# Hybrid attention and Fourier block on one core: form loads moved into the gate products, the modulation weight on GpSimd's queue, squares shared with VectorE, unread products in the start

## The chip, the core and the metric

The kernel runs on one core of one Trainium2 chip. Of its engines, TensorE (PE) multiplies matrices, VectorE (DVE) and ScalarE (ACT) work element by element, GpSimd (POOL) here does little besides issuing transfers, and SyncE (SP) only issues transfers. Each engine takes its instructions strictly in the order in which they stand, and semaphores hold an instruction back until its inputs are there. The metric is the time of one execution in microseconds. Before the change three runs took 1408.48, 1409.1 and 1411.9 us, a median of 1409.1 us.

## The reference

The reference is one layer over 512 latent tokens of width 2048, with 256 context tokens, in single precision:

```python
shift, scale, gate = jnp.split(silu_c @ w_ada[l] + b_ada[l], 3, axis=-1)
h = _modulate(_rmsnorm(xs, norm_g[l]), shift[:, None], scale[:, None])
...
p = h @ w_l
...
attn = _attention(q, jnp.concatenate([k, kc], axis=1), jnp.concatenate([v, vc], axis=1))
y = _merge(p[..., OFF_ZA:], attn, w_proj_a[l], w_proj_b[l], w_out[l])
new_xs = xs + gate[:, None] * y
...
return _rmsnorm(xs, final_g)
```

`_merge` holds the two sigmoid gates, each of width 2048, that multiply the projections of the attention branch and of the Fourier branch; the merged result goes through `w_o`.

## The kernel before

Every matrix product is made of three PE products (`mm3`, lines 219 to 223), because each operand is split into a high part, rounded by ACT (line 120, `whi` or `hh`), and the rest, subtracted by DVE (line 121, `wlo` or `hl`).

The order in which the instructions of an engine stand is not that of the text alone: the framework places the instructions of each engine when the program is built, by its own estimate of when inputs are there. A load that the text calls early can stand early or late in its queue, and a split can be placed ahead of another one. The places named below are those in the built programs.

The start (lines 336 to 465). SP loads x, transposed, in the pieces of `XCH`, then the modulation's weight `w_ss` (two pieces of 1 MB, `wada_load`, for each of 16 blocks `kb` of 128 channels, four buffers), and the first columns of `w_in` in small pieces (`w_start`). `squares` sums the squares of x: ACT squares two blocks, DVE adds them, PE sums over the channels with a matrix of ones (line 360). `rx` is the reciprocal root. `modulation(kb)` multiplies the conditioning vector with the weight on PE (`matvec`, line 387, two halves of 8 products), copies the sums out (`columns`, line 394), turns them with two transposes (line 397) and makes `shift` and `gain` of them (lines 399, 440, 441). `make_h` makes the block of h: `ht` on DVE (376), `hh` on ACT (377), `hl` on DVE (378). Then the products with `w_start` follow (`start_work`), 42 for each block.

The middle is the Fourier branch, the keys and values, and 48 steps of attention with other products between them (`fill`). During the attention `form_row` writes the forms to a scratch tensor in HBM, `f_d`: sums and differences of quarters of h, which the gate products need.

The gates (lines 988 to 1006). Each group of 512 gate columns is computed with seven products instead of eight of its quarters: `P1`, `Q5`, `P2`, `Q6`, `P7`, `Q3`, `Q4`, each of 4 weight pieces of 12 PE products. `P1` uses the weight in four buffers `R0` to `R3`, which SP loads; after its use further quarters are added onto `R` for the products `Q5`, `Q6` and `Q4`. For `Q5` SP loads the quarter into `wr` and DVE adds it (line 185); later ones are added by a transfer of GpSimd (line 194). `Q5` needs the form `Z5`, `Q6` `S2`, `P7` `S3` and `Q3` `S4`. The eight loads of the forms (four forms, two halves, 0.5 MB each, line 993) stand together on GpSimd's queue, ahead of the last `fill(64)`; each half is split between two pieces of the first group (`between`, line 59). The weights of `P2` in its second and third piece are split into `hh` and `hl` halves that the blocks of h no longer need.

The end (lines 1083 to 1206). The output product with `w_o` runs in the same seven products. `squares_of` collects the squares of the result in `ssq`, `rms` makes the reciprocal root of them, `scale_early` scales the first 256 tokens, and `last` does it for the last two blocks of 128 tokens. Line 1166 asks for the root function once, with no input that holds it back, so that its table is loaded at the start of the program.

Of the kernel before, what the change touches and what calls it, by code (L numbers as in the profile page):

```python
# [60 lines left out]
    f = {"P1": "Z5", "P2": "S2", "Q6": "S3", "P7": "S4"}.get(name)  # L61
    return [(f, pc - 1)] if f and g == 0 and pc in (1, 2) else []

XCH = [(0, 4), (4, 4), (8, 4), (12, 2), (14, 2)]


def start_pieces():
# [15 lines left out]
def block_kernel(ctx, tc, xT, ctxT, x, c_row, w_ss, w_gate, vecs, qkg, rope, dft_c, dft_s,  # L83
                 w_start, w_kv, w_m, w_g, w_pab, w_o, final_g, out):
    nc = tc.nc
# [23 lines left out]
    def uid(s):  # L109
        cnt[0] += 1  # L110
        return f"{s}{cnt[0]}"
# [218 lines left out]

    def wada_load(kb, h):
        w = pap.tile([P, 8, 256], F32, tag="wada", bufs=4, name=uid("wa"))
        nc.sync.dma_start(w, w_ss[kb, :, 8 * h : 8 * h + 8, :])
        return w

    for a, n in XCH:
# [14 lines left out]
    def squares(srcs, n, r, new, run=None):  # L351

        acc = bank2()
        for q in range(0, KK, 2):
            a, b = new(), new()
            for t, src in zip((a, b), srcs(q)):
                nc.scalar.activation(t, src, ACT.Square)
            nc.vector.tensor_tensor(a, a, b, op=ALU.add)
            if run is None:
                nc.tensor.matmul(acc[:, :n], ones, a, start=q == 0, stop=q == KK - 2)  # L360
            elif q == 0:
                nc.vector.tensor_copy(run, a)
            else:
                nc.vector.tensor_tensor(run, run, a, op=ALU.add)
        if run is not None:
            nc.tensor.matmul(acc[:, :n], ones, run, start=True, stop=True)
        nc.scalar.activation(r, acc[:, :n], ACT.Sqrt, bias=eps_t[:, 0:1], scale=1.0 / D)
        nc.vector.reciprocal(r, r)

    wada = {(0, 0): wada_load(0, 0), (0, 1): wada_load(0, 1)}  # L370
    while todo and len(ahead) < 3:
        start_load()

    def make_h(hi, lo, src, rr, kb, j, pool, n):
        tmp = pool.tile([P, n], F32, tag="htmp", bufs=2, name=uid("ht"))
# [12 lines left out]
                                 start=kk < 4, stop=kk >= KK - 4)  # L388
                kk += 1

    def columns(acc):

        o = pap.tile([P, 256], F32, tag="ada_o", bufs=2, name=uid("ado"))
        nc.vector.tensor_copy(o, acc[:, :256])
        sp = acc[:, 512:768]
        for i in range(2):
            nc.tensor.transpose(sp[:, P * i : P * i + P], o[:, P * i : P * i + P], ident)
        r = pap.tile([P, 2, 2], F32, tag="ada_r", bufs=2, name=uid("adr"))
        nc.vector.tensor_reduce(r, sp.rearrange("p (h g r) -> p h r g", h=2, g=4)[:, :, 0:2, :], axis=AX.X, op=ALU.add)
        return r  # L400

    def start_work():
        ends = {kb + nk for kb, nk in GROUPS}
# [31 lines left out]

    def modulation(kb):
        acc = bank2()
        matvec(acc, [wada.pop((kb, h), None) or wada_load(kb, h) for h in range(2)])
        sp = columns(acc)
        nc.vector.tensor_scalar(shift[:, kb, :], sp[:, 0, :], bada[:, kb : kb + 1], None, op0=ALU.add)  # L440
        nc.vector.tensor_scalar(gain[:, kb, :], sp[:, 1, :], bsc1[:, kb : kb + 1], ng[:, kb : kb + 1],
                                op0=ALU.add, op1=ALU.mult)

    rx = pap.tile([P, T], F32, name="rx")
    squares(lambda q: (xt[:, q, :], xt[:, q + 1, :]), T, rx, lambda: hm.tile([P, 2, T], F32, tag="h", name=uid("sq"))[:, 0, :])
    modulation(0)
# [522 lines left out]
    def slot(pool, shape, dt=F32):  # L969

        return pool.tile([P] + list(shape), dt, tag="h" if pool is hm else "f", bufs=KK, name=uid("s"))
# [17 lines left out]
    for i, f in enumerate(FORMS):  # L989
        forms[f] = [None] * 8  # L990
        for h in range(2):
            whole[f, h] = slot(fm, (4, 256)) if (i, h) < (3, 1) else new_ev().rearrange("p t (j c) -> p (t j) c", j=2)
            nc.gpsimd.dma_start(whole[f, h], f_d[i, :, 4 * h : 4 * h + 4, :])
    fill(64)
    pss.close()
    ps2 = ctx.enter_context(tc.tile_pool(name="ps2", bufs=1, space=PSUM, reuse_waits="tile"))
    for g in range(4):
        group = Group(g, forms, new_ev, gate_done, {"a": "x", "b": "y", "c": "x"})
        for name in ONE_GROUP:
            if (g, name) == (0, "Q5"):  # L1000
                hl_pools += range(MORE_HL)
            elif (g, name) == (3, "Q3"):
                raw_pools.pop()
            elif (g, name) == (3, "Q4"):
                hl_pools[:] = [p for p in hl_pools if not isinstance(p, int)]
            group.run(name)
# [74 lines left out]

    row = lambda l, j: l[j // 2][:, j % 2, None, :].broadcast_to([P, 2, 512])
    ssq = const.tile([P, 4, 5], F32, name="ssq")
    new_o = lambda: slot(fm, (2, 512))

    def squares_of(v, t, i):
# [76 lines left out]
        nc.vector.scalar_tensor_tensor(part(0), part(0), r, fgs[0][:, 0, :], op0=ALU.mult, op1=ALU.mult)  # L1163
        store(tok, 0)

    nc.scalar.activation(ssq[:, 0, 0:1], eps_t, ACT.Sqrt)
    nc.vector.memset(ssq, 0.0)

    jobs.insert(0, lambda: form("A22", 0))
    jobs += [lambda: load_rows(1), lambda: form("A12", 1), lambda: form("A22", 1)]  # L1170
# [21 lines left out]
    for name in ONE_GROUP:  # L1192
        if name == "Q5":
            jobs += [lambda: form("S2", 0), lambda: form("S2", 1)]
        elif name == "P2":
            jobs += [lambda: form("S3", 0), lambda: form("S3", 1)]
        elif name == "Q6":
            jobs += [lambda: form("S4", 0), lambda: form("S4", 1)]
        elif name == "Q3":
            prepare(last_group.X, 0, 1)  # L1200
        elif name == "Q4":
            prepare(last_group.Y, 1, 0)
        last_group.run(name)
# [84 lines left out]
```

## Time and profile before

| | |
|---|---|
| time of the runs, median (lowest to highest) | 1409.1 us (1408.48 to 1411.9) |
| the profiled execution's own time | 1406.39 us |
| its span | 1404.3 us |
| DVE busy | 896.2 us (64%) |
| ACT busy | 614.2 us (44%) |
| moved by DMA | 275.28 MB, a mean of 196 GB/s |
| PE in the chain that ended last | 89% of the span |

Times in the rows are microseconds from the start of the span. In the rows of the timeline stand the start, the time taken, the engine, the line of the kernel, the operation, what it writes and reads, how many instructions are put together, and in brackets how long the engine was idle before it and what ended that. In the windows stand the busy time of each engine (and its count of instructions), the granted clock of PE (1.00 is full speed), the busy share of the 16 DMA engines and what they moved. In the view of the waits stand the sum, the number and the longest one. PEld is the loading of a stationary operand on PE.

### The profile page before, as it was taken

The numbers are of one execution on the slowest core, as the hardware profiler recorded it, in microseconds if no ns is written. First come the engines' busy times: TensorE is split into PE (matmuls) and PEld (weight loads), VectorE is DVE, ScalarE is ACT, GpSimd is POOL, SyncE is SP. The second block draws the span as 40 slices with busy tenths as digits, with TensorE's granted clock in tenths as the row PEclk, the third lists the DMA queues.
The fourth block names the chain that finished last, engine by engine and source line by source line (L and its number), as shares of the span: only waits on it lengthen the run. The fifth ranks groups of instructions, "written<-read, shape, count | busy, mean of one in ns | idle before, by whom it ended". The sixth has DMA issues, their size and how long they took to land.

```text
span 1404.3 us, 17554 instructions
## 1 busy us (share of the span) xinstructions
PE 1358.6 (97%) x6842; PEld 1110.5 (79%) x6842; DVE 896.2 (64%) x1185; ACT 614.2 (44%) x837; POOL 91.6 (7%) x133
## 2 busy tenths in 40 slices
PE   6999999999999999999999699999999999999995
PEld 3667789888888888888887488888888888888874
DVE  4866596767866668666643767575866544437777
ACT  5322253534554444545553545453544333233544
POOL 0000000011100001000001000000010100000100
PEclk9999999999999999999999799999999999999998
DMA  9887553636543435434438898878898844244883
GB/s 367 323 322 269 189 168 121 183 120 184 165 143 99 134 113 155 130 99 127 136 119 324 252 258 232 262 226 240 284 265 304 326 151 137 87 135 152 181 230 127
DMA packets 73668, 275.28 MB, mean 196 GB/s; under 512 B 8433, under 2 KB 9073, under 8 KB 69105
## 3 DMA queue, kind: packets, MB, share of 16 engines
q1 hardware_dynamic: 56160, 212.54, 44.9%
q0 software_dynamic: 12240, 44.05, 13.1%
q10 hardware_dynamic: 5184, 17.57, 3.4%
q8 instruction: 53, 0.87, 0.3%
q14 instruction: 31, 0.25, 0.1%
HBM read 248.95 MB, written 25.17 MB: 195 GB/s over the span
## 4 chain that ended last, share of the span: by engine, by line
PE 89%; DMA 4%; DVE 3%; ACT 1%; issue 1%; SPq 0%; DVEq 0%; ACTq 0%
PE pb L221 12%; PE pb L222 12%; PE pb L223 12%; PE x L222 7%; PE x L223 7%; PE x L221 7%; PE y L223 6%; PE y L222 6%; PE y L221 6%; PE pd L221 3%; PE pd L223 3%; PE pd L222 3%; PE pd L916 2%; PE pd L387 2%; DMA wr<-in_w_g 2%
## 5 line engine op out<-in xcount | busy, mean ns | idle before, releaser
L121 DVE TENSOR_TENSOR wlo<-wr,whi 128x1024 fp32r<-128x1024 f32 x188 | 226.1, 1206 | 183.3 <-ACT whi L120 182.3
L120 ACT ACTIVATE whi<-wr 128x1024 fp32r<-128x1024 f32 x188 | 195.8, 1045 | 332.9 <-PE y L223 89.7
L221 PE MATMUL pb<-hh,whi 128*128 128x512 f32 x512 | 207.2, 407 | 2.3 <-ACT hh L377 2.3
L222 PE MATMUL pb<-hl,whi 128*128 128x512 f32 x512 | 201.8, 394 | 0.0
L223 PE MATMUL pb<-hh,wlo 128*128 128x512 f32 x512 | 201.4, 393 | 0.0
L222 PE MATMUL y<-wlo,s 128*128 128x512 f32 x348 | 135.9, 391 | 1.5 <-DVE wlo L121 1.5
L221 PE MATMUL y<-whi,s 128*128 128x512 f32 x348 | 135.9, 390 | 0.0
L223 PE MATMUL y<-whi,s 128*128 128x512 f32 x348 | 135.7, 390 | 0.0
L221 PEld LDWEIGHTS pb<-hh,whi 128*128 128x128 f32 x512 | 96.6, 189 | 23.2 <-ACT hh L377 3.4
L223 PEld LDWEIGHTS pb<-hh,wlo 128*128 128x128 f32 x512 | 96.4, 188 | 22.3 <-issue 1.7
L222 PEld LDWEIGHTS pb<-hl,whi 128*128 128x128 f32 x512 | 96.8, 189 | 18.0 <-issue 1.6
L222 PE MATMUL x<-wlo,s 128*128 128x512 f32 x248 | 96.9, 391 | 0.6 <-DVE wlo L121 0.6
L221 PE MATMUL x<-whi,s 128*128 128x512 f32 x248 | 97.1, 391 | 0.0
L223 PE MATMUL x<-whi,s 128*128 128x512 f32 x248 | 96.7, 390 | 0.0
L120 ACT ACTIVATE whi<-R 128x1024 fp32r<-128x1024 f32 x57 | 59.8, 1057 | 62.9 <-PE x L223 37.8
L121 DVE TENSOR_TENSOR wlo<-R,whi 128x1024 fp32r<-128x1024 f32 x57 | 69.2, 1221 | 25.8 <-ACT whi L120 25.8
L907 ACT ACTIVATE p<-pd,mx 128x768 f32<-128x768 f32 x48 | 43.1, 898 | 86.0 <-DVE mx L905 86.0
L222 PEld LDWEIGHTS y<-wlo,s 128*128 128x128 f32 x348 | 65.3, 188 | 16.4 <-DVE wlo L121 2.8
L221 PEld LDWEIGHTS y<-whi,s 128*128 128x128 f32 x348 | 65.3, 188 | 13.7
L223 PEld LDWEIGHTS y<-whi,s 128*128 128x128 f32 x348 | 65.3, 188 | 13.6
L121 DVE TENSOR_TENSOR ptl<-pd,pth 128x768 fp32r<-128x768 f32 x48 | 45.8, 954 | 30.1 <-ACT pth L120 30.1
L221 PE MATMUL pb<-whi,hh 128*128 128x512 f32 x144 | 57.1, 396 | 0.1
(278 smaller groups left out, 2687.1 us busy)
## 6 DMA issues: line engine op xcount, KB each, us to landing
wr<-in_w_g SPq DMA_DIRECT2D x80, 512.0 KB, 6.4
wa<-in_w_ss SPq DMA_DIRECT2D x32, 1024.0 KB, 7.8
wr<-in_w_m SPq DMA_DIRECT2D x44, 512.0 KB, 3.8
wr<-in_w_gate SPq DMA_DIRECT2D x32, 512.0 KB, 3.7
wr<-in_w_pab SPq DMA_DIRECT2D x32, 512.0 KB, 5.0
R<-in_w_g POOLq DMA_DIRECT2D x32, 512.0 KB, 9.2
wr<-in_w_o SPq DMA_DIRECT2D x32, 512.0 KB, 3.7
wr<-in_w_start SPq DMA_DIRECT2D x26, 512.0 KB, 6.6
```

Of the source, the lines that this page charges most:

```text
L120: nc.scalar.activation(hi, src, ACT.Copy)
L121: nc.vector.tensor_tensor(lo, src, hi.bitcast(F32), op=ALU.subtract)
L221: nc.tensor.matmul(o, ah, bh, start=start, stop=False, skip_group_check=cont)
L222: nc.tensor.matmul(o, ah, bl, start=False, stop=False, skip_group_check=cont)
L223: nc.tensor.matmul(o, al, bh, start=False, stop=stop, skip_group_check=cont)
L387: nc.tensor.matmul(acc[32 * j : 32 * j + 32, :256], c2[:, kk, :], w[:, k, :], start=kk < 4, stop=kk >= KK - 4)
L907: nc.scalar.activation(p, sc[:, :NKEY], ACT.Exp, bias=mx[:, 0:1], accum_out=mx[:, 1:2])
L916: nc.tensor.transpose(tp[:, k * P : (k + 1) * P], p[:, k * P : (k + 1) * P], ident)
```

## The change

1. x comes in six pieces instead of five, the first two of half the size.
2. The modulation's weight of blocks 2 to 15 is loaded on GpSimd's queue instead of SP's. The weight of block 1 is asked for beside that of block 0.
3. In the first stage three of the sixteen squares are made by DVE (a product with itself) instead of ACT. The sums leave PSUM through ACT instead of DVE (`columns`).
4. Eight PE products whose result nobody reads (`warm`) stand around the first modulation: three before its transposes, five after them.
5. The loads of `Z5` stay ahead of `fill(64)`; those of `S2`, `S3` and `S4` are asked for in the text at the start of `P1`, `Q5` and `P2`.
6. The table of the root function is asked for ahead of `Q3` of the output product, by an instruction that reads `ssq`; line 1166 goes, and `ssq` is cleared where it is allocated.

```diff
-XCH = [(0, 4), (4, 4), (8, 4), (12, 2), (14, 2)]
+XCH = [(0, 2), (2, 2), (4, 4), (8, 4), (12, 2), (14, 2)]
...
-        nc.sync.dma_start(w, w_ss[kb, :, 8 * h : 8 * h + 8, :])
+        (nc.gpsimd if kb > 1 else nc.sync).dma_start(w, w_ss[kb, :, 8 * h : 8 * h + 8, :])
...
-                nc.scalar.activation(t, src, ACT.Square)
+                if run is None and t is b and q in (4, 8, 10):
+                    nc.vector.tensor_tensor(t, src, src, op=ALU.mult)
+                else:
+                    nc.scalar.activation(t, src, ACT.Square)
...
-    wada = {(0, 0): wada_load(0, 0), (0, 1): wada_load(0, 1)}
+    wada = {(0, h): wada_load(0, h) for h in range(2)}
     while todo and len(ahead) < 3:
         start_load()
+    wada.update({(1, h): wada_load(1, h) for h in range(2)})
...
-        nc.vector.tensor_copy(o, acc[:, :256])
+        nc.scalar.copy(o, acc[:, :256])
         sp = acc[:, 512:768]
         for i in range(2):
             nc.tensor.transpose(sp[:, P * i : P * i + P], o[:, P * i : P * i + P], ident)
+        if kb == 0:
+            warm(5, o)
...
+    def warm(n, src):
+
+        for _ in range(n):
+            nc.tensor.matmul(wacc[:, :256], ones, src, start=True, stop=True)
...
-        matvec(acc, [wada.pop((kb, h), None) or wada_load(kb, h) for h in range(2)])
-        sp = columns(acc)
+        matvec(acc, pieces := [wada.pop((kb, h), None) or wada_load(kb, h) for h in range(2)])
+        if kb == 0:
+            warm(3, pieces[1][:, 7, :])
+        sp = columns(acc, kb)
...
+    wacc = bank()
...
-            whole[f, h] = slot(fm, (4, 256)) if (i, h) < (3, 1) else new_ev().rearrange("p t (j c) -> p (t j) c", j=2)
-            nc.gpsimd.dma_start(whole[f, h], f_d[i, :, 4 * h : 4 * h + 4, :])
+            if (i, h) < (3, 1):
+                whole[f, h] = slot(fm, (4, 256))
+
+    def load_form(i):
+        for h in range(2):
+            if (i, h) == (3, 1):
+                whole[FORMS[i], h] = new_ev().rearrange("p t (j c) -> p (t j) c", j=2)
+            nc.gpsimd.dma_start(whole[FORMS[i], h], f_d[i, :, 4 * h : 4 * h + 4, :])
+
+    load_form(0)
     fill(64)
...
         for name in ONE_GROUP:
+            if g == 0 and name in ("P1", "Q5", "P2"):
+                load_form(("P1", "Q5", "P2").index(name) + 1)
...
     ssq = const.tile([P, 4, 5], F32, name="ssq")
+    nc.vector.memset(ssq, 0.0)
...
-    nc.scalar.activation(ssq[:, 0, 0:1], eps_t, ACT.Sqrt)
-    nc.vector.memset(ssq, 0.0)
...
         elif name == "Q3":
+
+            nc.scalar.activation(mhalf[:, 8:9], ssq[:, 0, 2:3], ACT.Sqrt)
             prepare(last_group.X, 0, 1)
```

2 lines of the change are left out of this document (1 added, 1 removed).

## The prediction

> **What bounds the kernel now.** I read the page's head and its share of busy time first, then the list of waits of PE, then the windows, to see what each stage costs, and last the timeline of the three places where PE is not at full speed.
>
> ```profile
> span 1404.3 us, 17554 instructions
> PE 1358.6 (97%) x6842; PEld 1110.5 (79%) x6842; DVE 896.2 (64%) x1185; ACT 614.2 (44%) x837; POOL 91.6 (7%) x133
> ...
> PE x L221 <- ACT whi L120: 9.5, 2, 7.8
> ...
> PE x L222 <- DVE wlo L121: 7.4, 3, 6.0
> ```
>
> PE is busy for 1358.6 of 1404.3 us, so at most 45.7 us can be won without removing products or raising the clock. The waits (sum, number, longest) show that the two largest with a split at their end come to 16.9 us, and that single ones of 7.8 and 6.0 us make up most of it. The windows show where.
>
> ```profile
> 25.05:31.00 5.95, 5.95 (x26) 3.71 (x27) 1.87 (x4) 1.17 (x2) 0.00 (x0) 0.56 0.87 322
> ...
> 45.00:60.00 15.00, 14.91 (x98) 9.25 (x100) 13.17 (x25) 3.75 (x5) 0.00 (x0) 1.00 1.01 411
> ...
> 75.00:190.00 115.00, 115.00 (x737) 83.71 (x736) 70.34 (x121) 27.92 (x35) 0.00 (x0) 1.00 0.67 247
> ...
> 761.00:768.00 7.00, 5.67 (x26) 4.35 (x24) 1.82 (x2) 1.26 (x2) 0.00 (x0) 1.00 1.03 413
> 768.00:791.40 23.40, 8.46 (x23) 5.93 (x24) 19.19 (x19) 14.56 (x19) 0.90 (x1) 0.64 0.80 298
> ...
> 810.00:1000.00 190.00, 190.00 (x840) 157.30 (x839) 122.61 (x132) 92.73 (x113) 16.36 (x19) 1.00 0.87 248
> ```
>
> Columns are the stretch, its length, the busy time and count of PE, PEld, DVE, ACT and POOL, then the granted clock, the DMA share and GB/s. Between 75 and 190 us and between 810 and 1000 us PE is busy all the time at clock 1.00: nothing that only helps other engines there can shorten the kernel. Two stretches differ. From 25.05 to 31 us PE is busy but at a clock of 0.56. From 768 to 791.4 us it works 8.46 of 23.4 us, at 0.64, just after seven microseconds in which DMA was full (share 1.03). That second place is the start of the gates, and the largest thing to win. A PE product at full clock takes 190/840 = 0.226 us.
>
> **Forms and the first gate products (part 5).**
>
> ```profile
> 749.03 3.67 POOL L993 DMA_DIRECT2D s<-f_d  x7
> ...
> 761.07 0.39 PE L221 MATMUL x<-whi,hh 128*128 128x512 f32 x1
> ...
> 766.74 0.63 ACT L120 ACTIVATE hh<-wr 128x512 fp32r<-128x512 f32 x1 [5.77 <-DMA wr<-in_w_g]
> ...
> 770.45 1.15 ACT L120 ACTIVATE hh<-wr 128x512 fp32r<-128x512 f32 x2 [1.61 <-DMA wr<-in_w_g]
> ...
> 776.28 2.94 ACT L120 ACTIVATE s<-s 128x1024 fp32r<-128x1024 f32 x3
> 779.12 1.99 ACT L120 ACTIVATE whi<-R 128x1024 fp32r<-128x1024 f32 x2
> ...
> 784.60 1.23 DVE L185 TENSOR_TENSOR wr<-wr,wr 128x1024 f32<-128x1024 f32 x1 [1.82 <-DMA wr<-in_w_g]
> ...
> 785.74 1.22 DVE L121 TENSOR_TENSOR wlo<-R,whi 128x1024 fp32r<-128x1024 f32 x1
> ...
> 791.68 0.40 PE L221 MATMUL y<-whi,s 128*128 128x512 f32 x1
> ```
>
> P1 is 48 products, 48 × 0.226 = 10.9 us, and begins at 761.07. Q5's first product starts at 791.68, 30.6 us later, so 19.7 us are lost. The rows say how. ACT splits in order, and its split of R3 (`whi<-R`, 779.12) stands behind the splits of three halves of forms (`s<-s`, 776.28), which came late because seven form loads were issued together at 749.03. PE waited 7.8 us for that split. Then DVE's split of R3 (785.74) stood behind an addition of weights (784.60) that itself waited for a transfer, and PE waited 6.0 us more. Neither instruction ahead was needed for P1.
>
> The diff would spread the loads, but the built program does not: on GpSimd's queue seven of the eight form loads still stand together ahead of P1, and only the second half of `S4` moves, behind the four additions of line 194. So the burst of transfers stays; it even meets the stores of the forms' scratch a little sooner, and I charge 1 to 2 us of later landing for that. What does change is the order of the splits. On ACT, R3's `whi` now stands right behind the first of the `hh<-wr` splits and ahead of the other three and of `S2`. On DVE, R3's `wlo` stands ahead of the line 185 addition.
>
> ```profile
> L121 DVE TENSOR_TENSOR wlo<-wr,whi 128x1024 fp32r<-128x1024 f32 x188 | 226.1, 1206 | 183.3 <-ACT whi L120 182.3
> L120 ACT ACTIVATE whi<-wr 128x1024 fp32r<-128x1024 f32 x188 | 195.8, 1045 | 332.9 <-PE y L223 89.7
> ```
>
> A split costs 1.05 us on ACT and then 1.21 us on DVE. The replay: the first `hh<-wr` ended at 767.37 (766.74 + 0.63); with 1.2 us of delay 768.6. R3's `whi` ends at 769.6 and its `wlo` at 770.8. Line 221 needs the first, line 222 the second, so P1's last piece runs its second product at 770.8 and ends 11 products later, at 773.3, against 771.97 without a wait. Q5's first piece needs R0's new split, which on ACT stands behind the remaining three `hh<-wr` and the first half of `S2`. The last of these three ended at 771.6 before; 2 us later it is 773.6, then 2 × 1.05 us for `S2` and R0 gives 775.8, and DVE's 1.21 us gives 777.0. PE waits there about 3.4 us. Q5's third piece I let wait 0.8 us (its `whi` stands behind the second half of `S2`). Q5 then ends at 777.0 + 47 × 0.226 + 0.8 = 788.4. Before, it ended at about 791.68 + 10.9 = 802.6. That is 14.2 us.
>
> A wait of 3.4 us may bring the clock down. After a start with pauses the window from 25.05 shows 0.56 over 5.95 us, a loss of 0.44 × 5.95 = 2.6 us. I charge a dip as long as the wait that calls it, half of 3.4 us: 1.7 us; bounds 0 and 2.6. Remaining: 12.5 us. The bounds are 8 (the transfers come 4 us later still) and 19.7 (no wait left). The Trainium skill, "TensorE: Matmul & The Clock Gate", section "Part 1: The HAM clock gate (the "warmup" mystery)", says that activity is judged in free-running windows of about 3.4 us, an idle one bringing half rate and a busy one full rate. The trace agrees (0.56 and 0.64 stand behind its two idle places); by it alone the charge is either nothing or one window, an estimate of 1.7 us.
>
> The gain can only stay if later transfers keep up. From 810 to 1000 us the DMA share is 0.87 with PE never idle; 0.13 × 190 = 25 us of room, more than 12.5. So I expect no give-back.
>
> **The start (parts 1, 3, 4).**
>
> ```profile
> 6.22 2.19 ACT L357 ACTIVATE sq<-xt 128x512 f32<-128x512 f32 x4 [0.95 <-DMA xt<-in_xT]
> ...
> 8.15 9.63 PE L360 MATMUL pd<-sq,ones 128*128 128x512 f32 x16 [8.15 <-DVE sq L358]
> ...
> 17.82 0.69 ACT L367 ACTIVATE rx<-pd,eps_t 128x512 f32<-128x512 f32 x1 [2.38 <-PE pd L360]
> 18.53 3.35 DVE L368 RECIPROCAL rx<-rx 128x512 f32<-128x512 f32 x1 [2.38 <-ACT rx L367]
> ...
> 22.76 0.17 DVE L399 TENSOR_REDUCE adr<-pd 128x4 f32<-128x16 f32 x1 [0.59 <-PE pd L397]
> ...
> 23.43 0.75 DVE L376 SCALAR_TENSOR_TENSOR ht<-xt,gain,rx 128x512 f32<-128x512 f32 x1
> 24.10 1.22 DVE L121 TENSOR_TENSOR wlo<-wr,whi 128x1024 fp32r<-128x1024 f32 x1
> 24.28 0.72 ACT L377 ACTIVATE hh<-ht,shift 128x512 fp32r<-128x512 f32 x1 [2.49 <-DVE ht L376]
> 25.05 2.07 PE L221 MATMUL pb<-hh,whi 128*128 128x512 f32 x4 [2.33 <-ACT hh L377]
> 25.89 1.02 DVE L121 TENSOR_TENSOR wlo<-wr,whi 128x256 fp32r<-128x256 f32 x2
> ```
>
> A square costs 2.19/4 = 0.55 us on ACT and three leave it, 1.6 us; but the sums follow the arrival of x (the last ends at 17.78, ACT's root waits 2.38 us for it), and in the built order ACT loads the root's table within the squares instead of before them. So the root stays near 17.8 us, and the reciprocal still ends at 21.9. Behind it DVE has the chain sums, `gain`, `ht`. In the built order two splits that stood behind `ht` (24.10 and the pair at 25.89) now stand ahead of it: 1.22 + 1.02 = 2.24 us more, of which the time DVE idles there for PE's transposes takes back some; I put the first product at 26.4 instead of 25.05, a loss of 1.4.
>
> Against that stand three terms. In the wait PE does one half of block 1's `matvec`, whose weight now comes early: −1.07 (row below). The five unread products behind the transposes, which end at about 22.7 (the sum waits for them until 22.76), take 5 × 1.07/8 = 0.7 us or up to twice that at half clock and keep PE in use until about 23.8, so that of the 2.6 us of half clock some half goes: −1.2; by the skill's windows that would be none or one of them. And GpSimd's loads of block 2 share DMA with the rest of block 1 from about 18 us, which I charge with 0.4. Net 1.4 − 1.07 − 1.2 + 0.4 = −0.5; as the first product may come later still, I take −0.3. Bounds: all splits on the path and a colder clock, +3; no split on the path and all the clock, −1.07 − 2.6 + 1.4 = −2.3.
>
> **The modulation's weight on GpSimd's queue (part 2).**
>
> ```profile
> 42.76 1.07 PE L387 MATMUL pd<-wa,c 128*32 128x256 f32 x16
> ...
> 80.53 1.93 PE L387 MATMUL pd<-wa,c 128*32 128x256 f32 x32
> ...
> wa<-in_w_ss SPq DMA_DIRECT2D x32, 1024.0 KB, 7.8
> ...
> R<-in_w_g POOLq DMA_DIRECT2D x32, 512.0 KB, 9.2
> ```
>
> The two halves of a `matvec` (x16 each, two passes a product) cost 1.07 us when they stand apart, and 1.93 us together: 0.21 saved by each merge. In the built order there are 20 runs of them, not 25: 5 × 0.21 = 1.0 us. On GpSimd's queue nothing else of that time stands, so an issue that waits for a buffer holds up no one, and SP's loads of `w_start` no longer stand behind such an issue. PE has no wait to lose there. Moving the sums from DVE to ACT moves work to the engine that is busy 27.92 of 115 us in that stretch: nothing on the path. Bounds: −2 and the third rival.
>
> **The end (part 6).**
>
> ```profile
> 1386.83 1.28 ACT L1125 ACT_TABLE_LOAD   x1
> 1386.92 0.75 DVE L1152 TENSOR_TENSOR s<-y,s 128x256 f32<-128x256 f32 x2
> ...
> 1391.90 0.16 DVE L1124 TENSOR_REDUCE r<-ssq 128x1 f32<-128x5 f32 x1 [0.64 <-ACT s L1088]
> ```
>
> The table's 1.28 us leave the tail, but in the built order DVE's merge of `s` (1386.92), which ran beside that load, now stands behind the scaling of the first tokens that the load held up; the last square then ends near 1391.9 as now, and the reduction at 1391.90 moves by nothing. I take 0; bounds +0.3 and −1.28.
>
> **The sum.** −12.5 − 0.3 − 1.0 = −13.8. On the profiled execution's own 1406.39 us (span 1404.3 and 2.1 around it), which lies 2.7 below the median of the runs, that is 1392.6; on the median 1409.1 it is 1395.3 us.
>
> **The rivals.**
>
> First, part of the stall only moves. The line 185 addition (784.60) now stands ahead of the split of Q5's third piece. If its transfer lands as late as before, that split ends at 784.6 + 1.23 + 1.21 = 787.0 where PE wants it at 783.1: 3.9 us, and another dip of 1.7. Gain 13.8 − 5.6 = 8.2: 1401. For it: the burst of transfers is the same. Against it: their buffers come free sooner, as P1 ends sooner.
>
> Second, all that is lost goes: 19.7 us at the gates, 2.6 at the start, 1.0 of merges, 23.3 together: 1386. For it: no arithmetic forbids it. Against it: the burst is unchanged in the built order, and it alone lasts beyond P1's end.
>
> Third, slower than before: GpSimd's queue doesn't bring `w_ss` at the needed rate, and PE starves between 45 and 190 us. At 247 GB/s these 145 us want 35.8 MB. The gain is eaten once they take 13.8 us more, at 35.8/158.8 = 225 GB/s; at 215 GB/s they take 166.5, 21.5 more: 1395.3 + 21.5 = 1417. For it: transfers of half the size landed in 9.2 us from that queue against 7.8 from SP's. Against it: the window at 45 us moved 411 GB/s, and four buffers ask two blocks ahead. The Trainium skill, "DMA: Bandwidth & Descriptors", section "Queues, rings and completion order", says that each DMA engine takes turns between queues; by it SP's `w_start` gets half of what it had alone while both run, which speaks for this rival. No row of before has both queues loaded in that stretch.
>
> Fourth, the new order of splits isn't what decides: the transfers of R3 and of `wr` are, the 14 us stay, and the kernel does as before but for the merges and the start: 1408.
>
> **How the numbers follow.** The forecast has 0.60, the first rival 0.17, the second 0.07, the third 0.11, the fourth 0.05. Measurement tells 0.3% (4.2 us) from no change, so faster means below 1404.9. Forecast and the first two rivals lie there, 0.84, of which I move 0.01 to the others for spread; the fourth is the same, 0.05; the third slower, 0.11 and a mishap at the start beside it, 0.12 together. So 0.83, 0.05, 0.12. The range: the forecast's own is 1389 to 1400 by the bounds of the gates (8 to 19.7) and the start; it reaches up over the first rival to 1403.5 and leaves out the last two rivals and some of the second: 1388.5 to 1403.5.
>
> **What would show it.** Right: one wait of PE of 2 to 5 us at Q5's first piece instead of 7.8 and 6.0, Q5 ending 25 to 29 us after P1's start, against 41.5 before; `matvec` in 20 runs; first product of block 0 near 26.4; the reduction as far from the end as now. Wrong: PE waits for `wa` between 31 and 190 us (third rival); a wait of over 3 us on line 222 in Q5's third piece (first rival); R3's `whi` ending after 775 (fourth); form loads on GpSimd's queue held back in the run by something that the order doesn't show.

## The result, and the profile after

The changed kernel took a median of 1392.11 us in four runs (1391.06 to 1395.25), the kernel before beside it 1410.03 us (1408.48 to 1411.9). The ratio is 0.9876, with an interval of 0.9855 to 0.9897: 1.0 to 1.5% faster. The forecast was 1395.3 us in a range of 1388.5 to 1403.5. The profiled execution took 1392.62 us with a span of 1390.8, against 1404.3 before: 13.5 us less. By the medians the gain is more, 17.9 us where 13.8 was forecast, mostly because the profiled execution of the kernel before was 3.6 us faster than the median of its runs. The rows below account for the 13.5 us between the two profiles; a second profile of the changed kernel further down lies 17.6 us below the kernel before.

First the head of the page and the list of PE's waits of the changed kernel (sum, number, longest):

```profile
span 1390.8 us, 17626 instructions
PE 1358.8 (98%) x6858; PEld 1113.7 (80%) x6858; DVE 890.4 (64%) x1172; ACT 617.8 (44%) x849; POOL 106.6 (8%) x161
...
PE y L222 <- DVE wlo L121: 7.1, 5, 3.6
PE x L222 <- DVE wlo L121: 1.4, 2, 0.8
PE pb L221 <- ACT hh L381: 1.3, 1, 1.3
...
PE y L221 <- ACT whi L120: 0.6, 1, 0.6
```

PE is as long busy as before (1358.8 against 1358.6 us): the gain is idle time that went. The two waits of 7.8 and 6.0 us are gone. In their place stands one of 3.6 us on a `wlo`, for an accumulator `y`. The windows, with the columns as in the prediction:

```profile
25.00:31.00 6.00, 4.62 (x36) 2.53 (x29) 1.62 (x3) 2.68 (x5) 0.57 (x2) 1.00 1.02 419
...
768.00:791.40 23.40, 21.80 (x92) 17.16 (x93) 18.64 (x19) 16.39 (x18) 4.03 (x5) 1.00 1.05 329
791.40:810.00 18.60, 15.02 (x60) 11.95 (x59) 12.87 (x14) 9.27 (x11) 3.41 (x4) 0.91 0.84 231
```

The clock is 1.00 in the start, and PE works 21.80 instead of 8.46 us from 768 to 791.4 us. Part of the loss sits one window later now. The timeline there shows how:

```profile
758.15 0.39 PE L221 MATMUL x<-whi,hh 128*128 128x512 f32 x1
...
765.37 0.64 ACT L120 ACTIVATE hh<-wr 128x512 fp32r<-128x512 f32 x1 [2.46 <-DMA wr<-in_w_g]
765.91 1.04 ACT L120 ACTIVATE whi<-R 128x1024 fp32r<-128x1024 f32 x1
...
766.99 1.23 DVE L121 TENSOR_TENSOR wlo<-R,whi 128x1024 fp32r<-128x1024 f32 x1 [0.55 <-ACT whi L120]
...
772.86 0.50 PE L222 MATMUL y<-wlo,s 128*128 128x512 f32 x1 [0.76 <-DVE wlo L121]
...
785.25 1.06 ACT L120 ACTIVATE whi<-R 128x1024 fp32r<-128x1024 f32 x1
...
796.44 1.23 DVE L185 TENSOR_TENSOR wr<-wr,wr 128x1024 f32<-128x1024 f32 x1 [8.77 <-DMA wr<-in_w_g]
797.59 2.35 DVE L121 TENSOR_TENSOR wlo<-R,whi 128x1024 fp32r<-128x1024 f32 x2
...
798.86 0.50 PE L222 MATMUL y<-wlo,s 128*128 128x512 f32 x1 [3.58 <-DVE wlo L121]
...
811.26 0.39 PE L221 MATMUL x<-whi,s 128*128 128x512 f32 x1
```

R3's `whi` (765.91) stands right behind the first `hh<-wr`, and its `wlo` follows at 766.99, so P1 loses 1 us. Q5's first piece (second product at 772.86) loses 1.7 us, in waits of 0.55 and 0.76 us and the product between them. But Q6's first piece waits 3.58 us: its `whi` was ready at 786.3, and its `wlo` (797.59) stood on DVE behind an addition of two weights of P7 (796.44) that waited 8.77 us for a transfer. That is the mechanism which the prediction gave to its first rival, two of the seven products later than placed there (Q6 instead of Q5). Behind the wait PE's clock fell (0.91 in the window from 791.4): some nine products started 0.43 us apart instead of 0.23, which costs another 1.7 us.

A measure for the whole place: from P1's first product to P7's first stand 192 products, 192 × 0.227 = 43.6 us. Before they took 63.3 us (761.07 to 824.33), after 53.1 (758.15 to 811.26). The loss fell from 19.7 to 9.5 us. Of the 9.5, Q6's first piece has 5.5 (the wait and the clock), Q5's 1.8, P1's last piece 1.3; small delays make up the rest. The row of before:

```profile
824.33 0.39 PE L221 MATMUL x<-whi,s 128*128 128x512 f32 x1
```

The 13.5 us, in order of time: P1 begins 2.9 us sooner (761.07 to 758.15); 10.2 us at the gates; 1.2 us lost in the output product's P7, where PE's wait on line 222 grew; 1.7 us won behind the last product. For the last two the rows, first of the kernel before, then of the changed one:

```profile
1361.18 0.50 PE L222 MATMUL y<-wlo,s 128*128 128x512 f32 x1 [0.66 <-DVE wlo L121]
...
1389.37 9.83 SPq L1130 DMA_DIRECT2D out_y<-s  x14
...
1390.87 0.39 PE L223 MATMUL y<-whi,s 128*128 128x512 f32 x1
```

```profile
1347.02 1.23 DVE L185 TENSOR_TENSOR wr<-wr,wr 128x1024 f32<-128x1024 f32 x1 [6.36 <-DMA wr<-in_w_o]
1348.16 1.22 DVE L121 TENSOR_TENSOR wlo<-wr,whi 128x1024 fp32r<-128x1024 f32 x1
...
1349.43 0.50 PE L222 MATMUL y<-wlo,s 128*128 128x512 f32 x1 [1.88 <-DVE wlo L121]
...
1375.99 10.70 SPq L1155 DMA_DIRECT2D out_y<-s  x14
...
1379.08 0.39 PE L223 MATMUL y<-whi,s 128*128 128x512 f32 x1
...
1379.84 0.16 DVE L1149 TENSOR_REDUCE r<-ssq 128x1 f32<-128x5 f32 x1 [0.64 <-ACT s L1113]
```

The last product starts 13.4 us before the end in the kernel before and 11.7 in the changed one. The stores of the result begin 3.1 us ahead of it, against 1.5. At 1347 us the same pattern stands again: an addition that waits for a transfer, ahead of a split that PE wants.

### The profile page after: what moved, and what is told of

The parts are those of the page before. It is cut to its first block, busy times and chain, and to the rows that moved or that the text cites. A ratio compares the mean times of both kernels' runs of the same rounds, so it can differ in the third digit from the quotient of the medians.

```text
span 1390.8 us, 17626 instructions
## 1 busy us (share of the span) xinstructions
PE 1358.8 (98%) x6858; PEld 1113.7 (80%) x6858; DVE 890.4 (64%) x1172; ACT 617.8 (44%) x849; POOL 106.6 (8%) x161
## 4 chain that ended last, share of the span: by engine, by line
PE 89%; DMA 5%; DVE 4%; ACT 1%; issue 1%; DVEq 0%; SPq 0%; ACTq 0%
PE pb L221 12%; PE pb L222 12%; PE pb L223 12%; PE x L222 7%; PE x L223 7%; PE x L221 6%; PE y L222 6%; PE y L223 6%; PE y L221 6%; PE pd L221 3%; PE pd L223 3%; PE pd L222 3%; PE pd L930 2%; PE pd L391 2%; DMA wr<-in_w_g 2%; DVE wlo L121 1%
## 5 line engine op out<-in xcount | busy, mean ns | idle before, releaser
L222 PE MATMUL pb<-hl,whi 128*128 128x512 f32 x512 | 200.7, 392 | 0.1
## 6 DMA issues: line engine op xcount, KB each, us to landing
R<-in_w_g POOLq DMA_DIRECT2D x32, 512.0 KB, 10.1
```

The source lines that it names most:

```text
L222: nc.tensor.matmul(o, ah, bl, start=False, stop=False, skip_group_check=cont)
```

## The experiments

All were run beside the kernel before, whose median there was 1406.8 to 1407.7 us; so ratios to it are compared, also where two variants ran on different chips. Part 1, x in six pieces, was not tried alone. "Loss" is the time from the last product ahead of P1 to P7's first product less 0.227 us for each, taken from the trace (19.7 before, 9.5 in the changed kernel's first profile).

| kernel | us | ratio | interval | loss at the gates |
|---|---|---|---|---|
| changed kernel, again | 1388.74 | 0.9875 | 0.9860 to 0.9889 | 7.8 |
| before, with part 5 alone | 1394.03 | 0.9909 | 0.9892 to 0.9926 | 7.4 |
| part 5 undone | 1399.85 | 0.9941 | 0.9926 to 0.9957 | 17.4 |
| S3, S4 on SP's queue | 1389.36 | 0.9873 | 0.9853 to 0.9892 | 6.5 |
| part 6 undone | 1390.71 | 0.9880 | 0.9864 to 0.9897 | 7.9 |
| modulation's weight on SP | 1391.16 | 0.9887 | 0.9873 to 0.9902 | 7.3 |
| no unread products | 1391.57 | 0.9890 | 0.9874 to 0.9907 | 9.6 |
| nor their bank | 1391.71 | 0.9890 | 0.9875 to 0.9905 | 9.6 |
| part 3 undone | 1391.11 | 0.9885 | 0.9869 to 0.9902 | 7.6 |
| Q6's split ahead | 1386.94 | 0.9859 | 0.9844 to 0.9873 | 5.1 |
| three edits | 1384.83 | 0.9842 | 0.9828 to 0.9857 | 5.0 |
| the same, no unread products | 1388.72 | 0.9873 | 0.9858 to 0.9887 | 8.1 |

**The changed kernel again**

> The changed kernel itself, to stand beside the other three on the same chip: 0.987 to 0.989 of the kernel before. The loss around the first gate products (9.6 us in its first profile) and its places may differ from one execution to the next, as transfers land a microsecond sooner or later.

The ratio is the same, 0.9875. The loss was 7.8 us instead of 9.5: the wait at Q6 was 1.1 us instead of 3.6 there. So a difference of 2 us in this loss between two profiles says nothing by itself. The first product came at 25.6 us instead of 26.74, and the 588th, which is used below as a mark of the start, at 197.5 instead of 197.4.

**Part 5 alone, and all but part 5**

```diff
 kernel before:
+    load_form(0)
     fill(64)
...
+            if g == 0 and name in ("P1", "Q5", "P2"):
+                load_form(("P1", "Q5", "P2").index(name) + 1)
```

> The kernel before with part 5 alone (form loads asked for at P1, Q5 and P2). In its built program the splits around P1 stand in the same order as in the changed kernel: whi of R3 ahead of three of the four hh<-wr and of S2, wlo of R3 ahead of the line 185 addition of two wr. Theory A, that this order is the gain at the gates: 9 to 11 us faster than before, 1399 to 1401 us, PE's two waits of 7.8 and 6.0 us gone and one of 3 to 4 us at Q6's first piece (line 222), as in the changed kernel (19.7 us lost around the first products there, 9.6 after). Rival B, that part of the gain comes from the start or the queue of the modulation's weight (another phase of the clock, stores that leave sooner): less than 7 us faster, and a wait of more than 2 us still at R3.

The gain was 0.9%, 12.7 us by the medians (1406.76 to 1394.03), more than the 9 to 11 expected and close to the 12.5 that the prediction had summed for this part. The loss at the gates fell from 19.7 to 7.4 us, with the start and the queues of the kernel before, so rival B falls. Its waits:

```profile
PE y L222 <- DVE wlo L121: 3.2, 4, 1.4
...
PE x L221 <- ACT whi L120: 2.3, 1, 2.3
PE x L222 <- DVE wlo L121: 1.1, 2, 0.6
```

The reverse, in the changed kernel:

```diff
-    load_form(0)
+    for i in range(4):
+        load_form(i)
     fill(64)
...
-            if g == 0 and name in ("P1", "Q5", "P2"):
-                load_form(("P1", "Q5", "P2").index(name) + 1)
```

> The changed kernel with part 5 undone: all eight form loads ahead of the last fill(64), as before. In its built program whi of R3 stands again behind the four hh<-wr and the splits of S2 and S3. Theory A: 9 to 11 us slower than the changed kernel, 1401 to 1403 us, with PE waits of 6 to 8 us on whi<-R and 5 to 7 us on wlo<-R. Rival B: 1392 to 1397 us.

The size is theory A's: 17.4 us of loss at the gates against 7.8, and 0.0066 in the ratio, 9.3 us. The place is not what was expected, so this run doesn't confirm the mechanism. No split of R3 was waited for by 6 to 8 us; P1's very first product waited instead. Timeline of this run:

```profile
761.77 0.63 ACT L120 ACTIVATE hh<-wr 128x512 fp32r<-128x512 f32 x1 [6.05 <-DMA wr<-in_w_g]
...
765.39 1.99 ACT L120 ACTIVATE s<-s 128x1024 fp32r<-128x1024 f32 x2
...
767.28 1.54 ACT L864 COPY ev<-pb 128x512 f32<-128x512 f32 x3
...
768.87 0.79 PE L221 MATMUL x<-whi,hh 128*128 128x512 f32 x1 [12.89 <-ACT ev L864]
```

P1's accumulator waits for the copies of line 864 out of PSUM, which stand on ACT behind the `hh<-wr` that wait for a transfer and behind two splits of forms (`s<-s`). In the kernel before they stood there too, and no one waited. What differs is that the bank for the unread products (`wacc`) is taken ahead of all others. The likely account is that this moves the accumulators that are allocated later, and P1's now takes over a bank that those copies empty; the trace shows the copy that PE waits for and not the bank. (A run below takes the bank out of a variant that waits like this.) If so, part 4 put a wait into the program that only the new order of part 5 keeps short.

**The burst of transfers**

```diff
-            nc.gpsimd.dma_start(whole[FORMS[i], h], ...)
+            (nc.sync if i > 1 else nc.gpsimd).dma_start(whole[FORMS[i], h], ...)
```

> The changed kernel with the loads of S3 and S4 on SP's queue. ACT and DVE keep the order of the changed kernel, but three of these loads now stand behind P2's and P7's first weights and land later, so the burst of seven loads at 746 us is cut to four. Theory A, that the order of the splits sets the time: within 1.5 us of the changed kernel (1391 to 1394), and the wait at Q6's first piece stays, or grows because weights of P7 stand behind the forms. Rival C, that the burst itself still costs: R3 and the wr pieces land 3 us or more sooner, the waits of 0.6 to 0.8 us at R3 and at Q5's first piece go, 1387 to 1390 us.

0.9873 against 0.9875: theory A by the ratio. (1389.36 us would lie in rival C's range, but the changed kernel itself took 1388.74 when it was run again.) PE, ACT and DVE have exactly the order of the changed kernel. The loads of `S3` and the first half of `S4` were issued 11 to 15 us later, and the later pieces of weight landed sooner for it, the sixth at 769.2 instead of 773.3 us in the changed kernel run again. But the piece that ACT waits for first, the third, landed at 764.0 instead of 764.4. The wait at Q6 was 2.2 us, between the 1.1 and 3.6 of the changed kernel's two profiles. So the transfers did move as rival C says, the early ones least, and brought no time that can be measured. The order of the splits was the same in both, and so was the time.

**The table of the root (part 6)**

```diff
-            nc.scalar.activation(mhalf[:, 8:9], ssq[:, 0, 2:3], ACT.Sqrt)
...
+    nc.scalar.activation(ssq[:, 0, 0:1], eps_t, ACT.Sqrt)
+    nc.vector.memset(ssq, 0.0)
```

> The changed kernel with part 6 undone: the root's table is asked for at the start, and loaded anew in the end when the first root is wanted. By my forecast the chain up to the last sum of squares sets the end: same within 0.3 us. What the trace of the changed kernel shows instead: the first of the sixteen stores of the result starts 3.1 us ahead of the last product there and 1.5 us before, so the stores have drained when the last of them is issued: then 1.2 to 2 us slower with the part undone, 1393 to 1394 us, and the last store lands 5.8 us after the last scaling began instead of 4.3.

The ratios (0.9880 and 0.9875) don't differ beyond their intervals, though the median is 2.0 us higher (1390.71 against 1388.74). The traces show a smaller effect than expected: the last product starts 12.4 us before the end with the part undone, and 11.8 in both profiles of the changed kernel; 0.6 us. The last store lands 11.4 us after that product started against 10.8, which is these 0.6 us; in the eleven profiles with part 6 it lands after 10.5 to 10.9. The stores begin 1.5 us ahead of the last product, as in the kernel before:

```profile
1375.23 10.05 SPq L1154 DMA_DIRECT2D out_y<-s  x14
```

The 13.4 us of the kernel before, and of part 5 alone, are another 1.0 us longer. There the last store lands 11.7 us after the last product started, and the span goes on for 1.7 us behind that landing, against 1.0 with part 6 undone and in the changed kernel. So 0.27 us of it is the landing, and 0.76 lies behind all work. The 0.76 aren't part 6's: the run with the modulation's weight on SP, which has part 6, shows them too (1.7). In these three profiles one packet of the instruction queue arrives just before the end, and it doesn't in the changed kernel's two. The Trainium skill, "ScalarE: Activation LUTs", section "What ACT_TABLE_LOAD costs", gives 1.28 us for the load and 1.38 more for a drain. The trace has the 1.28 us, but no run here shows the drain, and the end came only 0.6 us sooner.

**The queue of the modulation's weight (part 2)**

```diff
-        (nc.gpsimd if kb > 1 else nc.sync).dma_start(w, w_ss[...])
+        nc.sync.dma_start(w, w_ss[...])
```

> The changed kernel with the modulation's weight of blocks 2 to 15 on SP's queue again (the weight of block 1 still asked for early). In the built program the matvec products stand in 23 runs, against 20 in the changed kernel and 25 before. Theory A, that GpSimd's queue brings only the merges (0.2 to 0.3 us each) and nothing waits for it: 0.5 to 1.0 us slower than the changed kernel. Rival D, that the queue itself is worth more since loads of w_start no longer stand behind weight loads that wait for buffers: 2 us or more slower, with PE waits in the first 75 us. Rival E, my third one in a small form, that two queues take bandwidth from each other: same or faster.

The ratio rose by 0.0012, within the intervals; by the medians the run is 2.4 us slower, which alone would fit rival D. The trace says that the start doesn't differ: of PE's products on lines 221 to 223 the 588th, by which all 16 blocks of `matvec` are done, started at 197.5 us in both, though one had 20 runs of `matvec` and the other 23. PE waits there for no weight, and once 0.5 us for a copy at 53 us. So neither the queue nor the merges are worth anything in the start that shows, and rival D falls with its place, the first 75 us; the 2.4 us are not explained. The Trainium skill, "DMA: Bandwidth & Descriptors", section "Queues, rings and completion order", has each DMA engine take turns between its queues; no run here shows a price of such turns in the start. The same product started at 200.7 us in the kernel before.

**The unread products (part 4)**

```diff
-        if kb == 0:
-            warm(3, pieces[1][:, 7, :])
...
-        if kb == 0:
-            warm(5, o)
```

> The changed kernel without the eight unread products. In its built program DVE makes ht of the first block right after gain, and the three wlo splits stand behind it, as before. Theory A, that the unread products pay by the clock: the granted clock falls to 0.5 to 0.7 somewhere between 22 and 31 us, the first product with w_start comes 1 to 2 us sooner (25 to 25.7 instead of 26.7), and the sum is 0 to 1.5 us slower than the changed kernel. Rival F, that they cost more than they pay, as they push ht behind the splits: the clock stays at 1.00 without them since block 1's weight is there early and keeps PE in use, and the kernel is 1 to 2 us faster.

The first product comes sooner and the clock dips, as theory A had it:

```profile
24.40 2.07 PE L221 MATMUL pb<-hh,whi 128*128 128x512 f32 x4 [3.40 <-ACT hh L381]
...
25.00:31.00 6.00, 6.00 (x34) 4.19 (x33) 1.26 (x3) 2.49 (x5) 0.53 (x1) 0.81 1.01 416
```

Both cancel: the 588th product starts at 197.3 us, against 197.5 with them. Yet the kernel is 2.8 us slower by the medians (1391.57 against 1388.74; the intervals overlap). Part of the loss lies 560 us later: P1's first product waits for the copy of line 864, and in all 1.8 us more are lost at the gates. Another 2.3 us of this profile lie in the output product's P7, whose wait is 3.1 us here and 1.1 in the changed kernel run again.

```profile
759.82 0.50 PE L221 MATMUL x<-whi,hh 128*128 128x512 f32 x1 [3.05 <-ACT ev L864]
```

So the next run took the bank away too.

```diff
-    wacc = bank()
```

> The changed kernel without the eight unread products and without the PSUM bank that is taken for them ahead of all others. Without the products alone the start was as fast by the 588th product (197.3 us against 197.5) and the kernel 2.8 us slower; there P1's first product waited 3.0 us for the last copy of line 864, whose bank its accumulator takes over. With the bank gone too, P1's accumulator lies in banks that transposes used, as in the kernel before. Theory H, that the slower time was the bank and not the clock: the wait at P1's start goes, and the time is that of the changed kernel within 1 us or better, 0.9865 to 0.988 of the kernel before. Rival A, that the unread products pay by the clock: 0.9885 to 0.99, as without the products alone.

The wait at P1's start went, as theory H says, which shows that the bank made it, but the time did not come back: 0.9890 again, and a loss of 9.6 us, now with 2.9 us at Q6's first piece and 1.4 at Q5's. The 588th product stood at 197.7 us. The pair below repeats it: 8.1 us are lost at the gates without unread products and 5.0 with them. In the three variants without them the loss is 8.1 to 9.6 us, in the eight profiles with them and part 5 it lies between 5.0 and 9.5; the kernel before with part 5 alone, which never had them, lost 7.4. Theory H isn't borne out as an account of the time; the intervals of 0.9890 and 0.9875 overlap, and those of the pair below don't. That the products pay by the clock of the start isn't shown either, since the start is as fast without them. Nor is a fall of the clock at the gates bound to their absence: five of the eight profiles with them have one, of 0.86 to 0.93 in the window from 768 or the one from 791.4 us. By what way they change the gates stays open.

**Q6's split ahead of the addition**

```diff
+            if e.key[:2] == ("P7", 0) and e.key[2] > 1:
+                nc.vector.scalar_tensor_tensor(src, src, zero, r, op0=ALU.add, op1=ALU.add)
...
+        if e.key == ("Q6", 0, 1):
+            nc.vector.tensor_scalar(zero, lo[:, 0:1].bitcast(F32), 0.0, None, op0=ALU.mult)
```

> The changed kernel in which the additions of two weights for the third and fourth piece of P7 (line 185) also add a zero that DVE makes of Q6's second split, so that DVE cannot take them ahead of Q6's first two splits; the result is the same. Theory A, that Q6's first piece waits only because DVE's split of R0 stands behind an addition that waits for a transfer: the wait of 3.6 us on line 222 there goes, and the clock's dip behind it: 3 to 5 us faster than the changed kernel. Rival G, that the transfers bound this stretch (DMA share 1.05 from 768 to 791 us), so that the stall only moves on to the first products of P7: within 1.5 us of the changed kernel.

Q6's `wlo` now come at 786.24, the addition at 797.28, and PE has no wait at Q6's first piece:

```profile
786.24 2.35 DVE L121 TENSOR_TENSOR wlo<-R,whi 128x1024 fp32r<-128x1024 f32 x2
...
793.53 0.39 PE L227 MATMUL y<-whi,s 128*128 128x512 f32 x1
793.75 0.39 PE L228 MATMUL y<-wlo,s 128*128 128x512 f32 x1
...
797.28 1.28 DVE L187 SCALAR_TENSOR_TENSOR wr<-wr,zero,wr 128x1024 f32<-128x1024 f32 x1
```

The loss is 5.1 us, 2.7 less than the changed kernel's on the same chip, and the time 1.8 us less (1386.94 against 1388.74; its slowest run is faster than the other's fastest). The mechanism is shown: with the order turned round the wait is gone. The expected 3 to 5 us were too many, because that wait was 1.1 us in that chip's trace and not 3.6. The rest of the 2.7 us is not the edit's: behind Q5's first piece the changed kernel's profile has some nine products at half rate, and this one has none. And 2.7 us went lost again in the output product's P7, where PE's wait was 2.6 us instead of 1.1 and the clock fell behind it.

**Three edits together**

```diff
-    wacc = bank()
     squares(...)
+    wacc = bank()
...
+            if e.key[:2] == ("P7", 0) and e.key[2] > 1 or e.key == ("P7", 4, 3):
+        if e.key in (("Q6", 0, 1), ("P7", 4, 2)):
```

> The changed kernel with three edits: the bank of the unread products is taken behind the first stage's sums, so that P1's accumulator lies as before; the zero of Q6's second split in the additions for P7's last two pieces of the first gate group; and the same for the addition for P7's last piece of the output product, behind which DVE's split of the third piece stood (PE wait of 1.9 us at 1349 us). Theory A: no wait at Q6's first piece nor in the output product's P7, 3 to 5 us faster than the changed kernel, 0.984 to 0.986 of the kernel before. Rival G, that transfers bound both places: 0.987 or more.

> As a_best, without the unread products and their bank. Theory H: like a_best within 1 us, as the products pay nothing by themselves. Rival A: 2 us or more slower than a_best.

0.9842 is the fastest, 22.9 us below the kernel before; it and the changed kernel run again, on another chip, are 3.9 us apart (0.9842 and 0.9875). What each of the three edits brings here was not tried, but for Q6's above. The largest wait at the gates and behind is 0.8 us:

```profile
PE y L228 <- DVE wlo L121: 2.9, 5, 0.8
PE x L228 <- DVE wlo L121: 1.5, 2, 0.8
```

Without the unread products it is 3.9 us slower, and the slowest of four runs with them is faster than the fastest without. The windows from 768 to 791.4 us, with and without them, show where the clock dips, and the rows show Q5's first product:

```profile
768.00:791.40 23.40, 21.81 (x94) 17.15 (x93) 20.10 (x21) 15.67 (x17) 5.73 (x7) 1.00 1.05 324
...
770.37 0.49 PE L227 MATMUL y<-whi,s 128*128 128x512 f32 x1 [0.83 <-ACT whi L120]
```

```profile
768.00:791.40 23.40, 20.26 (x77) 15.88 (x76) 19.11 (x19) 16.39 (x18) 4.88 (x6) 0.85 1.05 325
...
771.45 0.62 PE L227 MATMUL y<-whi,s 128*128 128x512 f32 x1 [2.50 <-ACT whi L120]
```

At the gates PE, ACT and DVE have the same order in both, so the order of the splits is not what differs. The transfer that the third `hh<-wr` waits for landed 1.1 us later without the products (768.3 against 767.2), Q5's first product waited 2.50 us instead of 0.83, and some fifteen products behind it ran at half rate. From P7 on the two take the same time to 0.2 us.

**Squares and sums on other engines (part 3)**

```diff
-                if run is None and t is b and q in (4, 8, 10):
+                if False:
...
-        nc.scalar.copy(o, acc[:, :256])
+        nc.vector.tensor_copy(o, acc[:, :256])
```

> The changed kernel with all squares of the first stage on ACT and the copy of the sums (columns) on DVE again, as before. DVE then makes that copy behind the reciprocal and ahead of the first split, so the transposes come some 1.5 us later. Theory I, that the start gained (3.3 us by the 588th product, where I forecast 1.3) because the copy on ACT lets the transposes and the first shift and gain come sooner: the 588th product comes 1 to 2 us later than in the changed kernel (198.5 to 199.5 us), and the kernel is 1 to 2 us slower. Rival J, that the gain is block 1's early weight, which fills PE's wait, and the clock: 588th product within 0.5 us of 197.5.

The 588th product comes at 199.1 us, 1.6 later, and the kernel takes 2.4 us longer by the medians, with intervals that overlap (0.9885 and 0.9875). Theory I's size holds, its mechanism for a part only. The waits of this run:

```profile
PE pd L391 <- DMA wa<-in_w_ss: 1.8, 1, 1.8
PE pd L401 <- DVE ado L398: 1.0, 1, 1.0
```

1.0 us is the copy that stands on DVE behind the reciprocal. 1.8 us is one wait for a piece of the modulation's weight, at 60 us, which the changed kernel doesn't have. Why that piece is late here wasn't tried.

## Why the prediction was right

**Direction and main cause hold; the close size is in part luck.** The forecast put 12.5 of 13.8 us at the gates and named the order of the splits, not the spreading of the loads. Part 5 alone brought 12.7 us, and with the order kept, other load times brought nothing. No run changed the order of R3's splits alone in the kernel before; for Q6 one did. The 13.8 us come near the 13.5 between the profiles because errors cancel: 2.3 us too many at the gates and 1.2 lost in the output product, against 1.6 too few up to P1's start and 1.7 at the end. By the medians the gain was 17.9, so 1392.11 us was 3.2 below the forecast, though well inside its range.

Of the signs that the prediction named, Q5 ended 25.9 us after P1's start (28.3 in the second profile; 25 to 29 forecast) and `matvec` stands in 20 runs. The wait at Q5's first piece came to 1.3 us instead of 2 to 5, and the reduction lies 11.0 us from the end instead of 12.4 as before.

**The gates, step by step.** One reading of the rows before was wrong: the halves of the forms were not late. ACT was never idle between 770.45 and 781.1 us, so no split of a form waited for its load; what held ACT was the transfers of `wr` (5.77 and 1.61 us) and then its own queue. The replay, which goes by the queue, isn't touched by it. R3's splits came where the replay had them: `whi` was to end 8.5 us after P1's start and `wlo` 9.7; they ended 8.8 and 10.1 us after it. Q5's first piece was to wait 3.4 us and waited 0.55 and 0.76: I had charged the landing of the last `hh<-wr` with 2 us and it came 1 us sooner than that. The 3.6 us at Q6 were not in the sum. The replay stopped at the end of Q5 and let every later wait stay hidden; the rival that named the mechanism looked for it in Q5. The 1.7 us that the prediction charged for a fall of the clock came true, behind the wait at Q6 and not the one at Q5. So the profile's gain there was 10.2 us instead of 12.5, within the bounds of 8 to 19.7. A row of before (784.60, an addition that waits ahead of a split) was the pattern, and it should have been followed through all products of the first group.

**The start and the merges: the sum was mis-sized, 1.3 us forecast, 3.3 measured by the 588th product.** The first product came at 26.74, as forecast (26.4). Its rows in the changed kernel:

```profile
19.44 3.35 DVE L371 RECIPROCAL rx<-rx 128x512 f32<-128x512 f32 x1 [3.72 <-ACT rx L370]
...
20.61 0.37 ACT L398 COPY ado<-pd 128x256 f32<-128x256 f32 x1 [1.21 <-PE pd L391]
...
25.12 0.75 DVE L380 SCALAR_TENSOR_TENSOR ht<-xt,gain,rx 128x512 f32<-128x512 f32 x1
...
26.74 0.73 PE L221 MATMUL pb<-hh,whi 128*128 128x512 f32 x2 [1.32 <-ACT hh L381]
```

The reciprocal began at 19.44 us, 0.9 later than before (17.83 in the second profile), where I had let it stay, and the five unread products behind the transposes took 2.3 us and not 0.7 to 1.4: I had priced them by a `matvec`, whose products start four at a time in the trace. But I had charged block 1's late weight and half of the clock's dip, and the clock stayed at 1.00 throughout. The merges, 1.0 us in the sum, showed nothing: 23 and 20 runs reach the 588th product at the same time. Part 3 was costed at nothing and is worth up to 1.6 us there; which part brings the other 1.7 was not tried. The right answer to the clock had a wrong reason as well: with the unread products the clock holds, and without them the start is as fast.

**The end was mis-sized, 0 forecast, 1.7 us measured.** The step took the last reduction for what sets the end. It moved by 0.3 us to the last product (1.03 before, 0.76 after), while the stores began 1.6 us sooner. Undoing part 6 gave back 0.6 of it. Another 0.27 is a sooner landing of the last store, whose cause stays open. The last 0.76 lie behind that landing and aren't part 6's.

**What was not seen.** With the bank of `wacc` P1's first product can wait for late copies out of PSUM (12.9 us in the run without part 5, 3.0 in one without the products; with the bank gone too, none). And 1.2 us went lost in the output product, where an addition on DVE waits 6.36 us for a transfer ahead of a split.

**The rivals.** The first, a stall that only moves, came true in a small form and in another place. The second is refuted (9.5 us of loss remain), the third too: PE waited for no piece of `w_ss` in the changed kernel's first profile and for less than 3 us in the second, all before 30 us. The fourth is refuted by part 5 alone.

## What to carry to other kernels

On an engine that works in order, look for the instruction that waits longest for a transfer and list what stands behind it; where one of these is wanted sooner than the waiting one's own result, the price can be the whole wait. Here DVE stood for 8.77 us and PE lost 3.6 of them. A data dependence of little cost can fix the order (here a zero that is added; making it took 0.15 us of DVE). Follow such a pattern through all stages that repeat it, not only the first.

A change that takes a PSUM bank early can make a product wait that stands much later in the program (3.0 us here, gone with the bank); before a run, see which copies the first product of each new stage waits for.

## What the runs showed that was not expected

Eight unread products at 20 us go with less loss at 770 us in both pairs of kernels (7.8 against 9.6, 5.0 against 8.1), while the 588th product comes within 0.2 and 0.7 us. The first difference is no larger than the one between two profiles of the changed kernel (9.5 and 7.8). The second goes with 3.9 us of the medians, and with the mean granted clock of all four runs: 0.997 or 0.998 with the products, 0.993 or 0.994 without. The landings at the gates vary by about 1 us between programs that issue them in the same order, and the clock dips to 0.85 in one of these kernels and holds 1.00 in the other. No run told apart whether this is the phase of the clock or the landings.

Equal pauses did cost different amounts. Q5's first piece waited 1.16 and 0.76 us in the changed kernel run again and 1.15 and 0.76 us with Q6's split ahead; behind it the one had some nine products at half rate, and the other none. The Trainium skill, "TensorE: Matmul & The Clock Gate", section "Part 1: The HAM clock gate (the "warmup" mystery)", has activity judged in windows that run free. Equal pauses could then cost a window or not, and this pair would fit that; no run here shows the windows themselves.
